# A two-layer DiT in split fp32: x loaded first, the first gate in the first phase, quarter sums of unsplit chunks, and the first values' projections interleaved part by part

## The chip, the cores and the metric

One core of a Trainium2 chip runs the whole program. The metric is the device time of one execution in microseconds. Five engines work side by side, each in its own fixed order: TensorE (PE) for matmuls, VectorE (DVE) and ScalarE (ACT) for element-wise work, GpSimd (POOL), and SyncE (SP), from whose queue the weights are loaded.

## The reference, cut to what matters

Two layers, each a half-step SwiGLU, a token mixer and another half-step SwiGLU, on 512 latent and 256 context tokens of width 1024 (768 rows in all). Each sub-layer takes the root mean square norm of its input and modulates it with shift and scale, and its result is multiplied by a gate; shift, scale and gate are products of a 1024-vector (`c` for latent, `c_ctx` for context tokens) with `ada_w`. All in float32.

```
def layer(x, xc, mod_l, mod_c, pre_wi, pre_wo, post_wi, post_wo, mixer, ctx_out):
    sh1, sc1, g1, sh2, sc2, g2, sh3, sc3, g3 = jnp.split(mod_l, N_MOD, axis=-1)
    ...
    def ffn_step(t, sh, sc, g, wi, wo):
        return t + 0.5 * g * swiglu(modulate(rms(t), sh, sc), wi, wo)

    x = ffn_step(x, sh1, sc1, g1, pre_wi, pre_wo)
    xc = ffn_step(xc, ch1, cc1, cg1, pre_wi, pre_wo)
    o_l, o_c = mixer(h_lat=modulate(rms(x), sh2, sc2), h_ctx=modulate(rms(xc), ch2, cc2), ctx_out=ctx_out)
    x = x + g2 * o_l
    x = ffn_step(x, sh3, sc3, g3, post_wi, post_wo)
    ...
for i in range(DEPTH):                      
    mod_l = (jax.nn.silu(c) @ ada_w[i] + ada_b[i])[:, None, :]
    mod_c = jax.nn.silu(c_ctx) @ ada_w[i] + ada_b[i]
```

## The kernel before

Activations are kept with the width on the partitions: x is 8 chunks (k) of 128 x 768, and a matmul takes a 128x128 piece of a weight as the stationary side and up to 512 tokens as the moving one. Every float32 matmul is done as three products of rounded parts: `h_h` with `whi`, `h_l` with `whi`, `h_h` with `wlo`. A slab of weights (`raw`, 128 x 1024, 512 KB, three places) is loaded through SP, cast on ACT (`whi`, line 73) and subtracted on DVE (`wlo`, line 74).

A feed-forward phase runs over 22 hidden blocks f. Blocks 0, 1 and 2 are plain (line 521): 96 matmuls for the two projections up, 48 of 512 columns and 48 of 256. From f=3 on seven products take the place of eight (class `Seven`, line 454), on sums of quarters of the activations (`T1`, `T2`, `T3`, made in `sums` at f=1) and of the weights (`s`, lines 440 to 443). In `sums` the two parts of a chunk are first added again (`both`, line 418), then the quarters are subtracted (`t`, lines 422 to 425) and split; `t4` replaces a quarter of the activations from f=3 on (`replace`).

Phase 0 starts cold. SP loads the vectors (`crep`, the two conditioning vectors on all partitions), x, and the modulation weights: shift for chunk k (`shift_job`, two sums of 128x1024 on DVE, line 182), scale (`scale_job`, on PE, lines 195 and 199), in one ring of nine places named `araw`. DVE and ACT make the norm (squares line 1117, adds line 1120), then `feed(k)` makes chunk k: product with `rall` (line 1134), modulation on ACT (line 1137), cast `h_h` (line 1138), `h_l` (line 1139), and PE multiplies block 0 chunk by chunk.

The gate of phase 0 (m=2), and all later modulations, are made by `Halves`: for half a column block (512) and chunk d, a load `wh` (line 237) and two sums of 128x512 on DVE (line 240), spread as steps over the hidden blocks from f=1 on; `beside(3, (5, 5, 6))` puts the gate's 16 steps into f=1, 2 and 3. The gate is needed first where phase 0's down projection is added to x (line 386).

In each attention the first projections read the norm's parts as they come out (blocks of 128 tokens, two of them a part of 256 columns): `qk` with heads 0 for all blocks, then `val` for all blocks in attention 0; `keys`, then `values`, in attention 1 (line 670 for the ones that start with the parts, line 657 for the rest). Each of them splits its weights' slabs into the ring of `whi`/`wlo` places.

A scheduler fixes the order of each engine when the program is built, by a model of costs, from the order in which the code is written and from which places are free; on the chip each engine runs that order, and waits for what it needs.

## Time and profile before

| | |
|---|---|
| median of 3 runs | 2842.01 us (2840.68 to 2843.09) |
| the profiled execution | 2840.03 us, span 2838.1 us, granted PE clock 0.987 |
| PE busy | 2701.7 us, 95% |
| DVE busy | 2185.6 us, 77% |
| ACT busy | 1207.4 us, 43% |
| POOL busy | 343.8 us, 12% |
| chain of work that ended last | PE 73%, DVE 14%, DMA 5%, ACT 3% |

The span is the time between the first and the last instruction in the trace; a little lies around it. The busy share is an average over the phases. The chain is followed back from the last instruction, at each step to what released it.

### The profile page before, as it was taken

Reading aid. Unit: us, or ns where it says so; the run is one execution under the profiler, and the core shown is the slowest. Engines: PE = TensorE matmul, PEld = TensorE weight load, DVE = VectorE, ACT = ScalarE, POOL = GpSimd, SP = SyncE. Lnnn points to the kernel's source line nnn. Section 1 sums busy time; section 2 is a strip of 40 time slices with the busy share of each in tenths; the row PEclk is TensorE's granted clock in tenths of the full one; section 3 lists DMA queues with packets and bytes.
Section 4 is the critical chain, followed back from the end, with each engine's and each line's share of the span. In section 5 each row is a group of like instructions: output and inputs, shape, how many; then the busy total and the mean of one; then the engine's idle time right before and its main releaser. Section 6 shows DMA issues by size and latency. Waiting matters only on the chain.

```text
span 2838.1 us, 47439 instructions
## 1 busy us (share of the span) xinstructions
PE 2701.7 (95%) x18028; PEld 2561.8 (90%) x18028; DVE 2185.6 (77%) x4727; ACT 1207.4 (43%) x2999; POOL 343.8 (12%) x468
## 2 busy tenths in 40 slices
PE   5799999989999889999999999999999999999999
PEld 4699998989999878999899989999998999899999
DVE  6988887886777768877787697777778666488887
ACT  4323332355655644332233352333235566444443
POOL 1000000043533421000000100000003421100000
PEclk9899999999999999999999999999999999999999
DMA  6433433321110142332333223432332101232333
GB/s 230 132 117 122 138 101 112 108 97 39 37 40 31 31 137 70 112 106 91 113 122 101 64 64 123 134 123 95 124 112 79 59 16 38 68 97 90 105 97 97
DMA packets 99284, 267.54 MB, mean 94 GB/s; under 512 B 12656, under 2 KB 16752, under 8 KB 98928
## 3 DMA queue, kind: packets, MB, share of 16 engines
q1 hardware_dynamic: 92544, 252.83, 27.8%
q10 hardware_dynamic: 6512, 11.68, 1.3%
q8 instruction: 142, 2.33, 0.3%
q14 instruction: 86, 0.70, 0.1%
HBM read 257.12 MB, written 7.34 MB: 93 GB/s over the span
## 4 chain that ended last, share of the span: by engine, by line
PE 73%; DVE 14%; DMA 5%; ACT 3%; issue 2%; POOL 1%; SPq 0%; ACTq 0%; POOLq 0%; DVEq 0%
PE ps_up L454 26%; PE ps_dn L568 22%; PE ps_qkv L657 7%; PE ps_up L521 5%; PE ps_dn L734 4%; DMA wh<-in_ada_w 3%; DVE wlo L74 2%; PE ps_av L995 2%; DVE wh L240 1%; DMA raw<-in_pre_wi 1%; PE ps_av L831 1%; PE ps_s L787 1%; DVE xs L369 1%; PE ps_pt L984 1%; DVE junkh L240 1%
## 5 line engine op out<-in xcount | busy, mean ns | idle before, releaser
L73 ACT CAST whi<-raw 128x512 fp32r<-128x512 f32 x556 | 341.0, 620 | 661.3 <-PE ps_dn L568 297.6
L568 PE MATMUL ps_dn<-ah,whi 128*128 128x256 f32 (+1 forms) x1456 | 464.6, 322 | 12.4 <-DVE x L386 10.7
L568 PE MATMUL ps_dn<-al,whi 128*128 128x256 f32 (+1 forms) x1456 | 461.9, 320 | 0.1
L568 PE MATMUL ps_dn<-ah,wlo 128*128 128x256 f32 (+1 forms) x1456 | 454.8, 319 | 0.2 <-DVE wlo L74 0.2
L74 DVE TENSOR_TENSOR wlo<-raw,whi 128x512 fp32r<-128x512 f32 x556 | 383.0, 693 | 77.2 <-ACT whi L73 59.6
L454 PE MATMUL ps_up<-h_h,whi 128*128 128x384 f32 (+1 forms) x1216 | 396.6, 326 | 23.0 <-ACT whi L73 16.5
L454 PE MATMUL ps_up<-h_l,whi 128*128 128x384 f32 (+1 forms) x1216 | 394.1, 324 | 0.0
L454 PE MATMUL ps_up<-h_h,wlo 128*128 128x384 f32 (+1 forms) x1216 | 393.3, 324 | 0.0
L386 DVE SCALAR_TENSOR_TENSOR x<-ps_dn,mod,x 128x256 f32<-128x256 f32 (+1 forms) x442 | 240.6, 554 | 129.6 <-PE ps_dn L568 104.8
L568 PEld LDWEIGHTS ps_dn<-ah,whi 128*128 128x128 f32 x1456 | 276.5, 191 | 35.8 <-ACT whi L73 8.2
L73 ACT CAST whi<-s 128x512 fp32r<-128x512 f32 x304 | 188.3, 620 | 272.2 <-PE ps_up L454 224.9
L568 PEld LDWEIGHTS ps_dn<-al,whi 128*128 128x128 f32 x1456 | 277.8, 191 | 19.6 <-DVE al L74 0.3
L568 PEld LDWEIGHTS ps_dn<-ah,wlo 128*128 128x128 f32 x1456 | 276.2, 191 | 20.4 <-DVE wlo L74 0.5
L454 PEld LDWEIGHTS ps_up<-h_h,whi 128*128 128x128 f32 x1216 | 230.4, 189 | 29.3 <-ACT whi L73 17.4
L74 DVE TENSOR_TENSOR wlo<-s,whi 128x512 fp32r<-128x512 f32 x304 | 208.0, 685 | 30.8 <-ACT whi L73 27.7
L454 PEld LDWEIGHTS ps_up<-h_h,wlo 128*128 128x128 f32 x1216 | 229.5, 189 | 1.9 <-DVE wlo L74 1.5
L454 PEld LDWEIGHTS ps_up<-h_l,whi 128*128 128x128 f32 x1216 | 230.3, 189 | 0.5
L657 PE MATMUL ps_qkv<-whi,h_h 128*128 128x256 f32 x704 | 204.6, 291 | 4.3 <-DVE a L613 3.6
L657 PE MATMUL ps_qkv<-wlo,h_h 128*128 128x256 f32 x704 | 199.8, 286 | 0.7 <-DVE wlo L74 0.7
L657 PE MATMUL ps_qkv<-whi,h_l 128*128 128x256 f32 x704 | 200.0, 285 | 0.0
L240 DVE SCALAR_TENSOR_TENSOR wh<-wh,ch 128x512 f32<-128x512 f32 x256 | 173.8, 690 | 19.5 <-DMA wh<-in_ada_w 19.3
L244 POOL TENSOR_TENSOR mod<-mod,part 128x16 f32<-128x16 f32 (+1 forms) x32 | 14.4, 450 | 1428.8 <-DVE wh L240 1428.8
(223 smaller groups left out, 6442.8 us busy)
## 6 DMA issues: line engine op xcount, KB each, us to landing
wh<-in_ada_w SPq DMA_DIRECT2D x256, 256.0 KB, 3.9
raw<-in_pre_wi SPq DMA_DIRECT2D x88, 512.0 KB, 3.5
raw<-in_post_wi SPq DMA_DIRECT2D x88, 512.0 KB, 3.5
raw<-in_pre_wo SPq DMA_DIRECT2D x44, 512.0 KB, 3.5
raw<-in_post_wo SPq DMA_DIRECT2D x44, 512.0 KB, 3.6
raw<-in_a_w_qk SPq DMA_DIRECT2D x16, 512.0 KB, 3.5
araw<-in_ada_w SPq DMA_DIRECT2D x8, 512.0 KB, 9.7
araw<-in_ada_s SPq DMA_DIRECT2D x8, 512.0 KB, 10.2
```

The source lines that it names most:

```text
L73: nc.scalar.copy(hi, src)
L74: nc.vector.tensor_sub(lo, src, hi.bitcast(F32))
L240: nc.vector.scalar_tensor_tensor(o, w, 1.0, self.c[ty], ALU.mult, ALU.mult, accum_out=self.part[:, ty, d:d + 1])
L369: nc.vector.scalar_tensor_tensor(xs, x[:, d, tk], sc, self.r[p], ALU.mult, ALU.mult)
L386: nc.vector.scalar_tensor_tensor(x[:, d, s0:s0 + n], ps, gate[ty][:, d:d + 1], x[:, d, s0:s0 + n], ALU.mult, ALU.add)
L454: nc.tensor.matmul(ps, ww, z[:, k, :n], start=first and k == 0 and i == 0, stop=k == 3 and i == 2, skip_group_check=True)
L521: nc.tensor.matmul(ps, w, h[:, k, s0:s0 + n], start=k == 0 and i == 0, stop=k == KC - 1 and i == 2)
L568: nc.tensor.matmul(ps, wv, a[:, s0:s0 + n], start=fi == 0 and k == 0, stop=fi == nf - 1 and k == 2)
L657: nc.tensor.matmul(ps, h[:, k, bt], w, start=n == 0, stop=n == 23)
L734: nc.tensor.matmul(ps, wv, o[:, k, s0:s0 + n], start=k == 0 and j == 0, stop=k == KC - 1 and j == 2)
L787: nc.tensor.matmul(sv[:, u], Q[:, c, qt], K[:, c, kb0 * P + u * half:kb0 * P + (u + 1) * half], start=i == 0, stop=i == 1)
L995: nc.tensor.matmul(po[:, j], a[:, k, j], V[:, kb, g], start=k == 0, stop=k == len(kbs) - 1)
```

## The change

SP loads the first half of x (512 columns) ahead of the conditioning vectors, and the second half behind them, then shift and scale of the first two chunks in turn. The gate m=2 leaves `Halves`: it is made by eight `vector_job`s, the former `shift_job` with m as an argument, each a load of 128x1024 and two sums of that width, written behind block 0 (`beside` at f=0). `Seven.sums` takes, in phase 0 alone, the modulated chunks `xr`, which still stand in their places unsplit, so the eight `both` adds are gone there, and `t4` is written over the first half of an `xr`. In the attentions `by_parts` puts the first values between the first queries and keys, two blocks at a time; the split weights of these values live in the places that later hold `aT` and `p` (`pT` in attention 1), under the name `vw`. Apart from these, the same instructions run.

```diff
--- before.py
+++ after.py
...
     class Slab:
-        def __init__(self, raw, room=(wp, 4)):
+        def __init__(self, raw, room=(wp, 4), places=None):
             self.parts = []
             for c in range(0, raw.shape[1], 512):
-                hi, lo = (room[0].tile([P, 512], F32R, name=z, tag=z, bufs=room[1]) for z in ("whi", "wlo"))
+                if places is not None:
+                    hi, lo = places.pop(0), places.pop(0)
+                else:
+                    hi, lo = (room[0].tile([P, 512], F32R, name=z, tag=z, bufs=room[1]) for z in ("whi", "wlo"))
                 split(hi, lo, raw[:, c:c + 512])
...
         return raw
-    def load_slab(src, pin=False):
-        return Slab(load_raw(src, pin))
+    def load_slab(src, pin=False, places=None):
+        return Slab(load_raw(src, pin), places=places)
+    def by_parts(f, g):
+        return [(h, 0, b) for p in range(0, NB, 2) for h in (f, g) for b in (p, p + 1)]
     other_banks("psf0")
...
         for ty, nm in enumerate(("c", "c_ctx")):
-            nc.sync.dma_start(crep[:, ty], I[nm].partition_broadcast(P))
+            keep(nc.sync.dma_start(crep[:, ty], I[nm].partition_broadcast(P)))
             nc.scalar.activation(crep[:, ty], crep[:, ty], AF.Silu)
...
     mods = [[None] * NMOD for _ in range(2)]
-    def shift_job(k, pool, crep, bufs):
+    def vector_job(m, k, pool, crep, bufs):
         w = pool.tile([P, D], F32, name="araw", tag="araw", bufs=bufs)
-        keep(nc.sync.dma_start(w, I["ada_w"][0, k]))
-        md = mods[0][0][2][:, :, k]
+        keep(nc.sync.dma_start(w, I["ada_w"][0, m * KC + k]))
+        md = mods[0][m][2][:, :, k]
         def sums():
...
                 nc.vector.scalar_tensor_tensor(o, w, 1.0, crep[:, ty], ALU.mult, ALU.mult, accum_out=md[:, ty:ty + 1])
-            nc.vector.tensor_add(md, md, adab[:, 0, k:k + 1].broadcast_to([P, 2]))
+            nc.vector.tensor_add(md, md, adab[:, 0, m * KC + k:m * KC + k + 1].broadcast_to([P, 2]))
+            if m == 2:
+                nc.vector.tensor_scalar_mul(md, md, 0.5)
         return sums
...
             self.cm.__exit__(None, None, None)
-        def sums(self, pool):
+        def sums(self, pool, full=None):
             n = self.n
-            self.t4 = [pool.tile([P, T], F32, name="t4", tag=tag, bufs=5) for tag in ("ah", "al")]
+            self.t4 = []
+            if full is None:
+                rooms = [pool.tile([P, T], F32, name="t4", tag=tag, bufs=5) for tag in ("ah", "al")]
             for k in range(KC // 2):
...
                 for i, tag in enumerate(("ah", "al")):
-                    r = pool.tile([P, T], F32, name="both", tag=tag, bufs=5)
                     kk = k + i * KC // 2
-                    nc.vector.tensor_add(r[:, :2 * n], self.hi[:, kk, :2 * n].bitcast(F32),
-                                         self.lo[:, kk, :2 * n].bitcast(F32))
+                    if full is None:
+                        r = pool.tile([P, T], F32, name="both", tag=tag, bufs=5)
+                        nc.vector.tensor_add(r[:, :2 * n], self.hi[:, kk, :2 * n].bitcast(F32),
+                                             self.lo[:, kk, :2 * n].bitcast(F32))
+                    else:
+                        r = full[kk]
                     b.append((r[:, :n], r[:, n:2 * n]))
                 t1, t2, t3 = (self.pool.tile([P, 512], F32, name="t", tag="s", bufs=4)[:, :n] for _ in range(3))
+                self.t4.append(rooms[k // 2][:, k % 2 * n:k % 2 * n + n] if full is None else b[1][0])
                 nc.vector.tensor_sub(t1, b[0][1], b[0][0])
...
                 nc.vector.tensor_sub(t3, b[1][1], b[0][1])
-                nc.vector.tensor_sub(self.t4[k // 2][:, k % 2 * n:k % 2 * n + n], b[1][0], t2)
+                nc.vector.tensor_sub(self.t4[k], b[1][0], t2)
                 for (th, tl), t in zip(self.T, (t1, t2, t3)):
...
             for k in range(KC // 2):
-                split(self.hi[:, k, n:2 * n], self.lo[:, k, n:2 * n], self.t4[k // 2][:, k % 2 * n:k % 2 * n + n])
+                split(self.hi[:, k, n:2 * n], self.lo[:, k, n:2 * n], self.t4[k])
         def up(self, pool, wg, wu, ah, al, first):
...
     EARLY = 1
-    def ffn(l, msh, w1, w2, nt, norm, pool, after_up, follow, side, beside=None, between=None, feed=None):
+    def ffn(l, msh, w1, w2, nt, norm, pool, after_up, follow, side, beside=None, between=None, feed=None, full=None):
...
             if f == PLAIN - 2:
-                seven.sums(pool)
+                seven.sums(pool, full)
             ah = pool.tile([P, T], F32R, name="ah", tag="ah", bufs=5)
...
             if pr_ not in vals:
+                places = None
+                if pr_ == 0:
+                    rooms = [pool.tile([P, 3 * 512], F32R, name="vw", tag="aT", bufs=2) for _ in range(2)]
+                    places = [r[:, c:c + 512] for c in range(0, 3 * 512, 512) for r in rooms]
+                    places += [pool.tile([P, T], F32R, name="vw", tag="p", bufs=5)[:, :512] for _ in range(2)]
                 vals[pr_] = (pool.tile([P, NB, 256], F32, name="V", tag="V", bufs=2),
-                             [load_slab(I["a_w_v"][pr_, half]) for half in range(2)])
+                             [load_slab(I["a_w_v"][pr_, half], places=places) for half in range(2)])
             V, slabs = vals[pr_]
...
             return (4, 5, 0, 1, 2, 3) if i else range(NB)
-        order = [(qk, 0), (val, 0), (qk, 1), (val, 1), (qk, 2), (qk, 3), (val, 2), (qk, 4), (qk, 5), (val, 3),
+        order = [(qk, 1), (val, 1), (qk, 2), (qk, 3), (val, 2), (qk, 4), (qk, 5), (val, 3),
                  (qk, 6), (qk, 7)]
-        proj = Projections([((f, i, b), lambda f=f, i=i, b=b: f(i, b)) for f, i in order for b in turns(i)], 2)
+        blocks = by_parts(qk, val) + [(f, i, b) for f, i in order for b in turns(i)]
+        proj = Projections([(fib, lambda fib=fib: fib[0](*fib[1:])) for fib in blocks], 2)
         later = Later()
...
             if b == 0:
-                qs_["v"] = [load_slab(I["b_w_kv"][1, half]) for half in range(2)]
+                rooms = [pool.tile([P, 5 * 512], F32R, name="vw", tag="pT", bufs=2) for _ in range(2)]
+                places = [r[:, c:c + 512] for c in range(0, 4 * 512, 512) for r in rooms]
+                qs_["v"] = [load_slab(I["b_w_kv"][1, half], places=places) for half in range(2)]
             nc.scalar.copy(V[:, b], project(b, hh, hl, qs_["v"]).rearrange("p (g d) -> p g d", g=4))
...
             nc.scalar.copy(O[:, 2 * g:2 * g + 2, qb * P:(qb + 1) * P], pt)
-        order = [(keys, 0, NB), (values, 0, NB)] + [(query, g, 4) for g in range(4)]
-        proj = Projections([((f, i, b), lambda f=f, i=i, b=b: f(i, b)) for f, i, n in order for b in range(n)], 1)
+        blocks = by_parts(keys, values) + [(query, g, b) for g in range(4) for b in range(4)]
+        proj = Projections([(fib, lambda fib=fib: fib[0](*fib[1:])) for fib in blocks], 1)
         later = Later()
...
     nc.scalar.activation(cvec, cvec, AF.Silu)
-    for m in range(2):
+    for m in range(3):
         md = const.tile([P, 2, KC], F32, name=f"mod0_{m}")
...
         load_small()
+        load_x(all_[0])
         crep = ada_vectors(start)
-        shifts = [shift_job(k, start, crep, FIRST) for k in range(2)]
+        load_x(all_[1])
         keep(nc.sync.dma_start(adab, I["ada_b"]))
-        for hf in range(2):
-            load_x(all_[hf])
-        scales = [scale_job(k, start, FIRST) for k in range(2)]
-        for f in shifts:
-            f()
+        first = [(vector_job(0, k, start, crep, FIRST), scale_job(k, start, FIRST)) for k in range(2)]
         xr = [pool.tile([P, T], F32, name="xr", tag=("ah", "al")[d % 2], bufs=5) for d in range(KC)]
...
                 step()
-        for f in scales:
-            f()
+        for z in first:
+            for f in z:
+                f()
         later = {}
...
             if k + 2 < KC:
-                later[k + 2] = [shift_job(k + 2, start, crep, FIRST), scale_job(k + 2, start, FIRST)]
+                later[k + 2] = [vector_job(0, k + 2, start, crep, FIRST), scale_job(k + 2, start, FIRST)]
             hi, lo = h0.reg.hi[:, k], h0.reg.lo[:, k]
...
             h1.open()
-        halves.add(0, (2,))
         halves.add(0, range(3, NMOD - 1))
-        others = halves.beside(3, (5, 5, 6))
+        others = halves.beside(3)
         def beside(f, seven):
             if f == 0:
+                for k in range(KC):
+                    vector_job(2, k, start, crep, FIRST)()
                 start_cm.__exit__(None, None, None)
...
                     others(f, seven)
-        ffn(0, 0, I["pre_wi"][0], I["pre_wo"][0], T, h0, pool, up_done, h1.follow, "right", beside, halves.between(13), feed)
+        ffn(0, 0, I["pre_wi"][0], I["pre_wo"][0], T, h0, pool, up_done, h1.follow, "right", beside, halves.between(13), feed, xr)
     o = attention_phase(0, h1, T)
```

Line numbers of the rows of the changed kernel below are those of its own file: line 190 there is line 182 before, 1161 is 1139, 570 is 554, 438 to 444 are 422 to 428.

SP's queue at the start of the program, before:

```order
L1096 DMA cvec<-in_cvec 128x16
L122 DMA crep<-in_c 128x1024
L122 DMA crep<-in_c_ctx 128x1024
L176 DMA araw<-in_ada_w 128x1024 x2
L1105 DMA adab<-in_ada_b 128x144
L129 DMA x<-in_x 128x4x512 x2
L129 DMA x<-in_x 128x4x256 x2
L190 DMA araw<-in_ada_s 128x1024 x2
L94 DMA raw<-in_pre_wi 128x1024 x2
L176 DMA araw<-in_ada_w 128x1024
```

and now:

```order
L1120 DMA cvec<-in_cvec 128x16
L137 DMA x<-in_x 128x4x512 x2
L130 DMA crep<-in_c 128x1024
L130 DMA crep<-in_c_ctx 128x1024
L137 DMA x<-in_x 128x4x256 x2
L1130 DMA adab<-in_ada_b 128x144
L184 DMA araw<-in_ada_w 128x1024
L200 DMA araw<-in_ada_s 128x1024
L184 DMA araw<-in_ada_w 128x1024
L200 DMA araw<-in_ada_s 128x1024
L97 DMA raw<-in_pre_wi 128x1024 x2
L184 DMA araw<-in_ada_w 128x1024
```

x moved ahead of the vectors and of the first `araw`; the same loads stand ahead of the first two `raw`. Behind them follow, as before, the other twelve `araw` of shift and scale, then now the eight of the gate, and only then the `raw` of block 1.

DVE from the last-but-one `h_l` of block 0 on, before (`sg` is the first gate-and-up product of block 0's result):

```order
L1139 TENSOR_TENSOR h_l<-xr,h_h 128x768
L201 SCALAR_TENSOR_TENSOR mod_1_95<-ps_b,adab 128x2
L1139 TENSOR_TENSOR h_l<-xr,h_h 128x768
L74 TENSOR_TENSOR wlo<-raw,whi 128x512 x2
L554 TENSOR_TENSOR sg<-sg,ps_up 128x512
L74 TENSOR_TENSOR wlo<-raw,whi 128x512
L418 TENSOR_TENSOR both<-h_h,h_l 128x768
L240 SCALAR_TENSOR_TENSOR junkh,part<-wh,ch 128x512
L554 TENSOR_TENSOR sg<-sg,ps_up 128x256
L74 TENSOR_TENSOR wlo<-raw,whi 128x512
```

and now, from the last `h_l` on, first piece:

```order
L1161 TENSOR_TENSOR h_l<-xr,h_h 128x768
L190 SCALAR_TENSOR_TENSOR araw,mod_2_96<-araw,crep 128x1024
L190 SCALAR_TENSOR_TENSOR junk,mod_2_96<-araw,crep 128x1024
L193 TENSOR_SCALAR mod_2_96<-mod_2_96 128x2
L191 TENSOR_TENSOR mod_2_96<-mod_2_96,adab 128x2
L190 SCALAR_TENSOR_TENSOR araw,mod_2_96<-araw,crep 128x1024
L193 TENSOR_SCALAR mod_2_96<-mod_2_96 128x2
L191 TENSOR_TENSOR mod_2_96<-mod_2_96,adab 128x2
L570 TENSOR_TENSOR sg<-sg,ps_up 128x512
L190 SCALAR_TENSOR_TENSOR araw,mod_2_96<-araw,crep 128x1024
L570 TENSOR_TENSOR sg<-sg,ps_up 128x256
```

and a few rows later (`sums` of the first quarter chunk, then the splits of block 1's weights):

```order
L74 TENSOR_TENSOR al<-sg,ah 128x512
L191 TENSOR_TENSOR mod_2_96<-mod_2_96,adab 128x2
L438 TENSOR_TENSOR t<-xr 128x384
L193 TENSOR_SCALAR mod_2_96<-mod_2_96 128x2
L74 TENSOR_TENSOR al<-sg,ah 128x256
L193 TENSOR_SCALAR mod_2_96<-mod_2_96 128x2
L439 TENSOR_TENSOR t<-xr,t 128x384
L440 TENSOR_TENSOR t<-xr 128x384
L438 TENSOR_TENSOR t<-xr 128x384
L444 TENSOR_TENSOR T1l<-t,T1h 128x384
L441 TENSOR_TENSOR xr<-xr,t 128x384
L74 TENSOR_TENSOR wlo<-raw,whi 128x512 x2
```

The splits of block 1's weights (`wlo` from `raw`) stood right behind the last `h_l`; now four sums of the gate, block 0's `sg` and `al` and the first quarter sums stand between. Twelve of the gate's sixteen sums stand ahead of the last `h_l`.

PE at the start of attention 0 (`ps_qkvs` are the first projections, `ps_qkv` the values', `ps_rt` a column sum of the norm), before:

```order
L670 MATMUL ps_qkvs<-whi,h_h 128x256
L670 MATMUL ps_qkvs<-whi,h_l 128x256
L670 MATMUL ps_qkvs<-wlo,h_h 128x256
L670 MATMUL ps_qkvs<-whi,h_h 128x256
L286 MATMUL ps_rt<-ones,ar 128x1 x2
L670 MATMUL ps_qkvs<-whi,h_l 128x256
L670 MATMUL ps_qkvs<-wlo,h_h 128x256
```

and now, about the same place:

```order
L686 MATMUL ps_qkvs<-whi,h_h 128x256
L686 MATMUL ps_qkvs<-whi,h_l 128x256
L686 MATMUL ps_qkvs<-wlo,h_h 128x256
L673 MATMUL ps_qkv<-vw,h_h 128x256 x2
L673 MATMUL ps_qkv<-vw,h_l 128x256
L673 MATMUL ps_qkv<-vw,h_h 128x256 x2
L673 MATMUL ps_qkv<-vw,h_l 128x256
L673 MATMUL ps_qkv<-vw,h_h 128x256 x2
```

The values' products, which stood behind all of the first queries and keys, now stand between them, in pieces of two blocks. In attention 1 the order on PE changes in the same way.

## Rows read from the trace of the kernel before

**Rows 1.** The page, part 1: busy us (share of the span) and instructions of each engine.

```profile
PE 2701.7 (95%) x18028; PEld 2561.8 (90%) x18028; DVE 2185.6 (77%) x4727; ACT 1207.4 (43%) x2999; POOL 343.8 (12%) x468
```

**Rows 2.** Busy time by stretch: stretch, length, PE, PEld, DVE, ACT, POOL, clock, DMA.

```profile
50.00:75.00 25.00, 24.12 (x137) 19.16 (x136) 12.60 (x26) 11.84 (x21) 0.00 (x0) 1.00 0.24 74
71.50:105.28 33.78, 33.78 (x194) 29.38 (x193) 33.48 (x75) 15.39 (x32) 0.40 (x1) 1.00 0.47 145
100.00:125.00 25.00, 9.17 (x53) 8.33 (x52) 24.58 (x61) 8.20 (x18) 0.40 (x1) 0.70 0.29 90
610.00:641.00 31.00, 26.31 (x199) 24.09 (x198) 28.64 (x70) 19.65 (x77) 17.01 (x20) 1.00 0.43 154
641.00:653.00 12.00, 12.00 (x103) 12.00 (x102) 3.67 (x8) 4.90 (x18) 5.08 (x7) 1.00 0.10 39
2168.00:2185.00 17.00, 12.85 (x93) 11.30 (x91) 16.72 (x38) 11.42 (x40) 9.33 (x13) 1.00 0.37 125
2185.00:2190.00 5.00, 5.00 (x29) 4.92 (x29) 5.00 (x14) 1.79 (x4) 0.92 (x2) 0.66 0.02 3
```

**Rows 3.** Timeline of SP's queue at the start: start us, us, instruction, count.

```profile
14.58 0.90 SPq L94 DMA_DIRECT2D raw<-in_pre_wi  x2
...
17.51 0.33 SPq L190 DMA_DIRECT2D araw<-in_ada_s  x1
18.97 0.33 SPq L176 DMA_DIRECT2D araw<-in_ada_w  x1
...
34.27 0.91 SPq L94 DMA_DIRECT2D raw<-in_pre_wi  x2
```

**Rows 4.** The page, part 6, DMA issues: count, KB each, median us to landing.

```profile
araw<-in_ada_w SPq DMA_DIRECT2D x8, 512.0 KB, 9.7
```

**Rows 5.** Timeline of DVE up to 70 us, idle before and its releaser in brackets.

```profile
24.96 1.97 DVE L74 TENSOR_TENSOR wlo<-raw,whi 128x512 fp32r<-128x512 f32 x3 [0.72 <-ACT whi L73]
...
33.31 1.22 DVE L182 SCALAR_TENSOR_TENSOR junk<-araw,crep 128x1024 bf16<-128x1024 f32 x1
34.46 0.08 DVE L182 DVE_READ_ACCUMULATOR junk<-araw,crep 128x1 f32 x1
...
34.60 3.55 DVE L1134 TENSOR_TENSOR xr<-x,rall 128x768 f32<-128x768 f32 x4
...
68.97 0.96 DVE L1139 TENSOR_TENSOR h_l<-xr,h_h 128x768 fp32r<-128x768 f32 x1 [2.24 <-ACT h_h L1138]
69.84 1.29 DVE L74 TENSOR_TENSOR wlo<-raw,whi 128x512 fp32r<-128x512 f32 x2
```

**Rows 6.** Timeline of DVE during block 1.

```profile
73.47 0.69 DVE L240 SCALAR_TENSOR_TENSOR junkh<-wh,ch 128x512 bf16<-128x512 f32 x1
74.08 0.09 DVE L240 DVE_READ_ACCUMULATOR junkh<-wh,ch 128x1 f32 x1
...
75.62 0.55 DVE L422 TENSOR_TENSOR t<-both 128x384 f32<-128x384 f32 x1
76.09 0.69 DVE L240 SCALAR_TENSOR_TENSOR junkh<-wh,ch 128x512 bf16<-128x512 f32 x1
...
77.92 2.69 DVE L418 TENSOR_TENSOR both<-h_h,h_l 128x768 f32<-128x768 f32 x3
```

**Rows 7.** Timeline of PE at the start of block 3.

```profile
105.28 0.34 PE L454 MATMUL ps_up<-h_h,whi 128*128 128x384 f32 x1
...
123.36 0.69 PE L454 MATMUL ps_up<-h_h,whi 128*128 128x384 f32 x1 [15.83 <-ACT whi L73]
...
127.36 0.34 PE L454 MATMUL ps_up<-h_h,wlo 128*128 128x384 f32 x1
```

**Rows 8.** Timeline of PE in attention 0: the longest of five waits, 610 to 641.

```profile
622.02 0.39 PE L670 MATMUL ps_qkvs<-whi,h_l 128*128 128x256 f32 x1 [1.19 <-DVE h_l L371]
```

**Rows 9.** Timeline of PE in attention 1: the two longest waits from 2168 on.

```profile
2174.80 0.39 PE L670 MATMUL ps_qkvs<-wlo,h_h 128*128 128x256 f32 x1 [1.59 <-DVE wlo L74]
...
2184.93 0.38 PE L670 MATMUL ps_qkvs<-whi,h_l 128*128 128x256 f32 x1 [1.47 <-DVE h_l L371]
```

## The prediction

> **What bounds the kernel now.** I read the busy times of the engines first. TensorE (PE) works for 95% of the span [rows 1], so nearly all the time that can be won lies in the few stretches where PE waits, and the next view is the busy time by stretch of time [rows 2]. It shows three such places that the change touches. Between 100 and 125 us PE is busy for 9.17 of 25 us at a granted clock of 0.70. Between 610 and 641 us, where attention 0 begins, it is busy for 26.31 of 31 us (4.7 us idle), and then for all of the next 12 us. Between 2168 and 2185 us, where attention 1 begins, it is busy for 12.85 of 17 us (4.15 us idle), and the 5 us behind that run at a clock of 0.66. The remaining waits are elsewhere, and the change leaves them alone.
>
> The timeline of PE shows the first place closely [rows 7]: the third hidden block ends at 105.28, the seven-product block f=3 issues 12 matmuls, then PE idles for 15.83 us until 123.36, and the next 12 matmuls take until 127.36: 4.0 us, where the twelve before the wait took 2.1, so 1.9 us at half clock (1.2 instead of 2.4 GHz) come on top. The wait ends with an ACT cast of a sum of weights, and VectorE (DVE), which makes that sum, is busy for 24.58 of those 25 us [rows 2]: it is late. Yet it was idle for 12.4 of the 25 us between 50 and 75 [rows 2], in pauses of which the last, 2.24 us, stands ahead of the last `h_l` [rows 5]. So DVE has the time, only before it has the work.
>
> **The change, part by part.**
>
> *x first.* Up to the first weights the queue moves the same bytes in another order, and these weights are waited for: their DMA issued at 14.58 [rows 3], the first `wlo` began at 24.96 [rows 5]. I cost the new order at nothing: the squares and sums of x get done in DVE's pauses before 24.96, and the `h_l` stand behind the splits of these weights anyway. If the first weights landed earlier or later, all of phase 0's start would move with them, by 1 us at most, I estimate, since loads of 512 KB are issued some 1.5 us apart there [rows 3].
>
> *The gate in whole rows.* 32 halves of 128x512 become 16 sums of 128x1024. A half takes 0.61 us until the next instruction starts (73.47 to 74.08) [rows 6], a whole row 1.15 (33.31 to 34.46) [rows 5]: 16 x 1.15 = 18.4 us for 32 x 0.61 = 19.5, so 1.1 us of DVE less. [...]
>
> What matters is where they stand. In the new order 12 of the 16 stand ahead of the last `h_l`, 4 behind it and ahead of the next block's splits (order at DVE above). From 24.96, where DVE is free, to the end of the last `h_l` it now has 4 splits (2.6 us, 0.66 each), 24 sums of 128x1024 (27.6), 8 products with `rall` (7.1 by 3.55 for four), 8 `h_l` of the same shape (7.1) [rows 5] and some 1.6 us of small ones: 46.0, so it ends at about 71.0 instead of 69.84. It no longer pauses. PE's products of block 0 end 1.7 us later.
>
> *Block 1 then waits.* Before, the splits of block 1 came right behind the last `h_l`, at 69.84 [rows 5], and PE ran on: it was busy for all of the 33.78 us from 71.5 to 105.28 [rows 2], which are the two blocks 1 and 2 with 96 matmuls each, so f=0 ended near 71.5. Now the order has 4 sums of the gate (4.6 us), two `sg` and two `al` (1.9), six operations of the quarter sums 128x384 (2.8 by 0.47, which is the step from 75.62 to the next row at 76.09), some 0.3 of small ones and one split (0.6) between them [rows 5, 6]: 10.2 us behind 71.0, so the first `wlo` is ready at 81.2. PE can do two products before it, so block 1 effectively begins at 80.9: 9.4 us late. PE's wait of some 8 us will drop the clock, as the 15.83 us did [rows 7]; I take the same 1.9 us.
>
> *The stall at f=3 goes.* Behind that point DVE has no half sums of the gate in f=1 and f=2 (they took 19.5 us), no `both` adds (8 x 0.9 = 7 us by the three in 2.69) [rows 6], and in its order the sums `s` of the weights stand ahead of the end of block 2. So f=3 goes on without its wait. DVE's slack for this: it was busy for 33.48 of the 33.78 us of blocks 1 and 2 and for 24.58 of the 25 up to 125 [rows 2], and 26 us of that are now gone or done earlier. Startup: 15.83 + 1.9 won, 9.4 + 1.9 lost, so 6.4 us. Bounds: all 17.7 us if block 1 isn't late, 0 if it is late by 15.8.
>
> *First values part by part, attention 0.* Before, the values' 96 matmuls run alone from 641 to 653, with DVE busy for 3.67 of 12 us, and PE's waits, five, come before that, the longest for an `h_l` [rows 2, 8]. Now values stand between the keys' products on PE (order at PE above), and they need only the same `h_l`. DVE's own work before 653 is 28.64 + 3.67 = 32.3 us, PE's 26.31 + 12.0 = 38.3: with the two side by side PE is the bound, and up to 4.7 us go. The four splits of the values' weights (2.6 us) now come earlier on DVE, in front of `h_l`s. The waits at the very start (one split, one `h_l`) are only partly covered, since the first values come just there. I take 3.6, bounds 0 and 4.7.
>
> *Attention 1.* The same with keys and values: 4.15 us of idle time, with 1.59 and 1.47 us as the longest waits [rows 9], and 5 us at a clock of 0.66, which is worth 1.7 us [rows 2]. I take three quarters of both, 4.4; bounds 0 and 5.9.
>
> *Elsewhere* the order of PE, DVE and SP is the same or differs by a few rows under a busy PE: nothing.
>
> Sum: 6.4 + 3.6 + 4.4 = 14.4 us. The profiled execution took 2840.03, so 2825.6; the median of the three runs is 2.0 us above it: **2827.6 us**.
>
> **The rivals.**
>
> (a) *Block 1 isn't late.* If block 1's start holds and f=3's wait goes, startup wins 17.7 and the sum is 26: 2816. For it: 12.4 idle us of DVE could hold most of the 18.4 us of the gate. Against it: the order is fixed, and nothing in it pulls the splits forward.
>
> (b) *The startup's gain is eaten.* Block 1 starts at 87 instead of 81, because block 0 starves PE in between, at half clock, or ACT's casts (`sg`, `ah`, `T1h`) answer late, as DVE's pause for `h_h` shows it can [rows 5]. Then startup gives 0 and 8.0 stay: 2834.
>
> (c) *The attentions don't fill.* If `h_l` remains what PE waits for, with the values' splits in front of it, the idle time only changes place: 2836 with the startup's 6.4 alone, and 2842, as before, together with (b).
>
> (d) *Slower: the gate's loads.* Each waits on SP for a place of `araw`, and the weights of block 1 stand behind all eight on that queue. A load of this kind takes 9.7 us from issue to landing in the startup [rows 4]. If each landed before the next was issued, seven from 34.27 [rows 3] would end at 102, the last `h_l` near 104.5 and block 1 would begin at 115. The case decides from a start at 101: 87.3, where f=3's old stall is used up, plus the attentions' 8.0, plus 5.7; so it gives 5.7 + 14, 2862. Against it: issues stand 1.5 us apart (17.51 and 18.97) while a load takes 9.7 [rows 3, 4], so they overlap, and the places come free from about 45 on. [...]
>
> **How the numbers follow.** Differences within 0.2% (5.7 us, 2836.3 to 2847.7) can't be told from no change. Chances: the forecast 0.50 (2822 to 2832), (a) 0.13, (b) 0.13, (c) alone 0.12, (b) and (c) together 0.05, (d) 0.07. Faster: 0.50 + 0.13 + 0.11 of (b) + 0.07 of (c) = 0.81; same: the rest of (b), (c) and both together, 0.12; slower 0.07. The range 2817 to 2838 leaves out (d), the double case and the outer parts of (a) and (c), about 0.2.
>
> **What would show it.** Right: no wait of PE near 107, and one of 7 to 9 us at the start of block 1, ended by `wlo` or `whi`; DVE without pauses from 25 to 80; PE idle for less than 1.5 us behind 610 and 2168 each. Wrong: block 1 at or before 73 (a); the 13th matmul of f=3 at 123 or later (b); waits for `h_l` of the old size (c); DVE waiting for DMA ahead of a sum of the gate (d).

## The result, and the profile after

The changed kernel took 2823.35 us (median of four runs, 2820.59 to 2823.57) beside 2841.35 us for the kernel before (2839.78 to 2843.09): a ratio of 0.9930 with a 95% interval of 0.9919 to 0.9942, so 18 us or 0.7% faster. The forecast was 2827.6. Of all the runs below one, the fourth of e_gate_again, took 3287.64 us at a granted clock of 0.751; it stands in no median here. The profiled execution took 2823.49 us, its span is 2821.3. The busy times of the engines, in the order of [rows 1] (busy us, share of the span, instructions), hardly moved:

```profile
PE 2705.1 (96%) x18028; PEld 2565.6 (91%) x18028; DVE 2176.2 (77%) x4703; ACT 1205.7 (43%) x2995; POOL 339.3 (12%) x464
```

PE issues the same 18028 matmuls, and what changed is where it waits. Busy time by stretch, in the columns of [rows 2]:

```profile
50.00:75.00 25.00, 19.03 (x115) 14.74 (x112) 25.00 (x57) 10.55 (x18) 0.00 (x0) 1.00 0.47 169
75.00:100.00 25.00, 18.37 (x81) 15.22 (x82) 22.33 (x54) 10.73 (x23) 0.00 (x0) 0.80 0.21 64
100.00:125.00 25.00, 25.00 (x151) 22.80 (x150) 13.35 (x25) 9.96 (x20) 0.00 (x0) 1.00 0.19 66
...
610.00:645.00 35.00, 35.00 (x294) 34.90 (x294) 26.64 (x65) 18.67 (x80) 17.10 (x24) 0.99 0.36 132
...
2162.00:2185.00 23.00, 22.02 (x181) 21.35 (x180) 21.43 (x50) 15.26 (x53) 10.44 (x13) 1.00 0.31 97
```

Between 50 and 75 us DVE was idle for half of the time before and is now busy without a gap; PE fell from 24.12 to 19.03 there. Between 100 and 125 us it is the other way round: PE, which was busy for 9.17, runs through, and DVE has 11.65 us to spare. The stall moved from block 3 to blocks 0 and 1 and became shorter. In the two stretches of the attentions PE now has next to no gap; in attention 0 two waits stand just ahead of that stretch (below).

The timeline of PE at the start (start, duration, matmul, in brackets the idle time ahead of it and what ended that) shows the new waits, and f=3 without one:

```profile
69.42 0.50 PE L537 MATMUL ps_up<-h_l,whi 128*128 128x512 f32 x1 [3.36 <-DVE h_l L1161]
...
72.72 0.50 PE L537 MATMUL ps_up<-h_l,whi 128*128 128x512 f32 x1 [0.92 <-DVE h_l L1161]
...
80.92 0.79 PE L537 MATMUL ps_up<-h_h,whi 128*128 128x512 f32 x1 [6.54 <-ACT whi L73]
...
83.28 0.79 PE L537 MATMUL ps_up<-h_h,wlo 128*128 128x512 f32 x1 [0.71 <-DVE wlo L74]
...
118.73 0.34 PE L470 MATMUL ps_up<-h_h,whi 128*128 128x384 f32 x1
...
120.82 0.34 PE L470 MATMUL ps_up<-h_h,whi 128*128 128x384 f32 x1
```

The last row is f=3's thirteenth matmul, ahead of which PE waited 15.83 us before [rows 7]. It now comes 2.09 us behind the first, and 2.54 us earlier than before, although block 1 starts with a wait.

DVE in the same place (timeline, answers to [rows 5, 6]):

```profile
69.28 1.22 DVE L190 SCALAR_TENSOR_TENSOR araw<-araw,crep 128x1024 f32<-128x1024 f32 x1
70.42 0.08 DVE L190 DVE_READ_ACCUMULATOR araw<-araw,crep 128x1 f32 x1
...
71.71 0.95 DVE L1161 TENSOR_TENSOR h_l<-xr,h_h 128x768 fp32r<-128x768 f32 x1
72.58 1.22 DVE L190 SCALAR_TENSOR_TENSOR araw<-araw,crep 128x1024 f32<-128x1024 f32 x1
...
82.54 1.28 DVE L74 TENSOR_TENSOR wlo<-raw,whi 128x512 fp32r<-128x512 f32 x2
```

No row there has an idle time in front: the splits of block 1's weights start 9.96 us behind the last `h_l`, and all of that is work. PE's wait of 6.54 us itself ends with ACT's cast of these weights, `whi`. In ACT's order that cast stands behind the casts of block 0's result and of the first quarter sum, and these wait for DVE, where the gate's sums come first (timeline of ACT):

```profile
77.01 0.62 ACT L73 CAST ah<-sg 128x512 fp32r<-128x512 f32 x1 [2.44 <-DVE sg L570]
78.49 0.40 ACT L73 CAST ah<-sg 128x256 fp32r<-128x256 f32 x1 [0.86 <-DVE sg L570]
79.84 0.51 ACT L443 CAST T1h<-t 128x384 fp32r<-128x384 f32 x1 [0.94 <-DVE t L438]
80.25 1.14 ACT L73 CAST whi<-raw 128x512 fp32r<-128x512 f32 x2
```

So the gate's sums hold up block 1 twice, by ACT's queue and, 0.71 us more, by DVE's own splits. In SP's queue (timeline) the gate's loads are not what is late:

```profile
44.12 12.41 SPq L184 DMA_DIRECT2D araw<-in_ada_w  x8
56.58 1.51 SPq L97 DMA_DIRECT2D raw<-in_pre_wi  x3
```

All eight are issued by 56.58, and block 1's weights right behind them, 26 us ahead of their split; each of these three loads landed within 7.0 us of its issue.

At the two attentions these are the waits of PE that are left up to 645 and from 2156 to 2185 (timeline), against [rows 8, 9]:

```profile
605.62 0.39 PE L686 MATMUL ps_qkvs<-whi,h_h 128*128 128x256 f32 x1 [1.60 <-ACT whi L73]
607.49 0.58 PE L686 MATMUL ps_qkvs<-wlo,h_h 128*128 128x256 f32 x1 [1.37 <-DVE wlo L74]
...
2163.91 0.38 PE L686 MATMUL ps_qkvs<-wlo,h_h 128*128 128x256 f32 x1 [0.47 <-DVE wlo L74]
2167.44 0.51 PE L673 MATMUL ps_qkv<-vw,h_h 128*128 128x256 f32 x2 [0.43 <-DVE vw L74]
```

The waits for `h_l` are gone from both. Those for the first weights stayed: in attention 1 they are shorter (0.47 us instead of 1.59 for `wlo`, and 0.43 for `vw`), in attention 0 they are 2.97 us together, where before there was one (timeline of PE, before):

```profile
612.41 0.39 PE L670 MATMUL ps_qkvs<-wlo,h_h 128*128 128x256 f32 x1 [0.91 <-DVE wlo L74]
```

The two of attention 0 do not hang on the new order: with the old one there (e_att0, below) they are 0.99 and 1.37 us.

Where the time came from is read by following one instruction of PE that both programs have through both traces: f=3's first matmul, the first matmul of the down projections (`ps_dn` behind f=3), the first norm sum behind phase 0 that PE waits for, each attention's first output product, and the last matmul. Start times in us; the last two columns are experiments below.

| | before | after | after, second execution (e_again) | gate back (e_gate) |
|---|---|---|---|---|
| f=3, first matmul | 105.28 | 118.73 | 117.52 | 103.76 |
| f=3, thirteenth | 123.36 | 120.82 | 119.60 | 105.84 |
| first down product | 147.99 | 143.85 | 142.61 | 129.83 |
| norm sum behind phase 0 | 602.07 | 596.21 | 598.40 | 587.68 |
| output product, attention 0 | 1012.33 | 1003.32 | 1002.75 | 988.87 |
| norm sum ahead of attention 1 | 2157.59 | 2146.78 | 2147.06 | 2132.63 |
| output product, attention 1 | 2415.23 | 2396.68 | 2398.36 | 2382.45 |
| last matmul | 2834.67 | 2817.74 | 2818.41 | 2801.17 |

From the second column against the first: 4.1 us won at the first down product, 5.9 by the end of phase 0, 3.2 more across attention 0 (410.26 to 407.11), 1.8 up to attention 1, 7.7 across its start (257.64 to 249.90), and 1.6 lost behind: 16.9 in all.

One pair of executions says little of a single segment, and the thirteen traces of this case say more. Attention 0, from the norm sum to its output product, takes 400.7 to 407.1 us, 403.4 on average, in the ten with the new order there, and 409.8 to 411.8, 410.6 on average, in the three with the old one (before, e_start, e_att0). Attention 1 takes 249.8 to 254.2, 251.5 on average, in the ten with the new order, and 257.6 to 260.7, 259.1 on average, in the three with the old one (before, e_start, e_att1). In these segments the new order is worth 7.2 and 7.6 us; the attention 0 of the first profile of after is the longest of its ten.

### The profile page after: what moved, and what is told of

Its sections match the earlier page's. It is cut to its first block, busy times and chain, and to the rows that moved or that the text cites. A ratio compares the mean times of both kernels' runs of the same rounds, so it can differ in the third digit from the quotient of the medians.

```text
span 2821.3 us, 47391 instructions
## 1 busy us (share of the span) xinstructions
PE 2705.1 (96%) x18028; PEld 2565.6 (91%) x18028; DVE 2176.2 (77%) x4703; ACT 1205.7 (43%) x2995; POOL 339.3 (12%) x464
## 5 line engine op out<-in xcount | busy, mean ns | idle before, releaser
L673 PE MATMUL ps_qkv<-whi,h_h 128*128 128x256 f32 x608 | 177.8, 292 | 3.2 <-DVE a L629 2.2
L250 DVE SCALAR_TENSOR_TENSOR wh<-wh,ch 128x512 f32<-128x512 f32 x240 | 163.4, 693 | 18.3 <-DMA wh<-in_ada_w 18.2
L673 PE MATMUL ps_qkv<-wlo,h_h 128*128 128x256 f32 x608 | 174.1, 286 | 0.7 <-DVE wlo L74 0.7
L673 PE MATMUL ps_qkv<-whi,h_l 128*128 128x256 f32 x608 | 173.6, 286 | 0.0
```

Source lines behind the costliest of these rows:

```text
L250: nc.vector.scalar_tensor_tensor(o, w, 1.0, self.c[ty], ALU.mult, ALU.mult, accum_out=self.part[:, ty, d:d + 1])
L673: nc.tensor.matmul(ps, h[:, k, bt], w, start=n == 0, stop=n == 23)
```

## The experiments

Theory after the result: the stall at f=3 went because DVE has less to do there; the gate's sums, which stand ahead of block 1's splits, cost most of what that wins; and each attention's order is worth what its segment shows. Rivals: the gate's move is what removed the stall; x first did part of it; the attentions' gains are drift. Each run below changes the changed kernel, and its time stands beside runs of the kernel before on the same chip (medians 2843.97, 2842.56 and 2844.34 in the three groups).

**Both attentions in the old order (e_start).**

```diff
-        order = [(qk, 1), (val, 1), (qk, 2), ...
+        order = [(qk, 0), (val, 0), (qk, 1), (val, 1), (qk, 2), ...
-        blocks = by_parts(qk, val) + [(f, i, b) for f, i in order for b in turns(i)]
+        blocks = [(f, i, b) for f, i in order for b in turns(i)]
...
-                qs_["v"] = [load_slab(I["b_w_kv"][1, half], places=places) for half in range(2)]
+                qs_["v"] = [load_slab(I["b_w_kv"][1, half]) for half in range(2)]
-        blocks = by_parts(keys, values) + [(query, g, b) for g in range(4) for b in range(4)]
+        blocks = [(f, 0, b) for f in (keys, values) for b in range(NB)] + [(query, g, b) for g in range(4) for b in range(4)]
```

(`val` of the first heads takes the common places too.)

> The changed kernel with both attentions in the old order (values behind all of the first queries and keys, their splits in the ring of whi/wlo), so the change at the start alone. If the three places add up as the traces of before and after show them (5.8 us at the end of phase 0), this is about 5.9 us faster than before, 2835.5. If part of the 18 us came by chance of the granted clock in later phases, it lies off that by more than 1.5 us.

Measured: 2833.75 us (2827.73 to 2839.97), ratio to before 0.9961 [0.9947, 0.9975]. The startup alone is faster than before, and the two attentions together are worth 10.4 us against the changed kernel's 2823.35 (8.8 by the ratios, 0.9961 less 0.9930). The time lies 1.75 us below the expected 2835.5, just beyond the 1.5 us that were allowed; with runs of this one kernel 12 us apart that decides nothing about the clock.

**Attention 0 alone in the old order (e_att0).** The edit is the first half of the one above.

> The changed kernel with the old order in attention 0 alone. The prediction has 3.6 us for attention 0, so 2827.0; the cumulative lead in the two traces grows by 6.4 us over the start of attention 0 and falls by 3.3 towards its end, so 2826.5 to 2828; if what PE wins at the start is all given back later in the attention, 2823.4, as the changed kernel.

Measured: 2826.71 us (2822.74 to 2833.19), ratio 0.9942 [0.9925, 0.9959]: 3.4 us more than the changed kernel's 2823.35, where 3.6 was forecast, but 6.3 more than its 2820.37 (e_again), and 7.0 less than e_start in the same group, which is attention 1's share. With runs 10 us apart the time alone does not settle the size; the segments above, 411.79 us here against 403.4 on average, put it nearer 7. In its trace a wait for `h_l` and the one for the norm's `y` are back at the old size (timeline of PE, e_att0):

```profile
616.21 0.38 PE L686 MATMUL ps_qkvs<-whi,h_l 128*128 128x256 f32 x1 [1.18 <-DVE h_l L381]
...
625.47 0.66 PE L657 MATMUL ps_t<-ident,y 128*128 128x128 f32 x4 [1.04 <-POOL y L648]
```

**The gate back beside its halves (e_gate).** x first, unsplit sums and the attentions stay.

```diff
-    for m in range(3):
+    for m in range(2):
...
+        halves.add(0, (2,))
         halves.add(0, range(3, NMOD - 1))
-        others = halves.beside(3)
+        others = halves.beside(3, (5, 5, 6))
...
-                for k in range(KC):
-                    vector_job(2, k, start, crep, FIRST)()
```

> The changed kernel with the gate m=2 back in Halves (32 half sums in blocks 1 to 3); x first, quarter sums of unsplit chunks and the attentions stay. Theory of the prediction: the gate's sums ahead of the splits cost 9.4 us at block 1 and the quarter sums alone take most of the stall at block 3 away (7 us of both adds gone, and the first sums fit into DVE's pauses in block 0), so without the gate's move the start is shorter: no wait of PE at block 1, one of about 4 us at block 3, 2818 (2815 to 2822). Rival: the gate's move is what removes the stall at block 3; then the stall comes back with 12 us or more and the time is 2828 or above.

Measured: 2807.96 us (2804.02 to 2812.0), ratio 0.9874 [0.9859, 0.9889]: faster than the changed kernel by 15 us, well beyond what was expected. The theory's direction holds, but the wait of 4 us that it left at block 3 is not there, and the rival falls: the stall at f=3 does not need the gate's move to go away. f=3's first and thirteenth matmul (timeline of PE, e_gate):

```profile
103.76 0.34 PE L470 MATMUL ps_up<-h_h,whi 128*128 128x384 f32 x1
...
105.84 0.34 PE L470 MATMUL ps_up<-h_h,whi 128*128 128x384 f32 x1
```

PE by stretch in e_gate:

```profile
50.00:75.00 25.00, 22.81 (x128) 17.87 (x127) 18.23 (x40) 16.14 (x30) 0.00 (x0) 1.00 0.22 74
75.00:100.00 25.00, 25.00 (x145) 21.74 (x144) 24.03 (x59) 9.47 (x19) 0.22 (x1) 1.00 0.46 146
100.00:125.00 25.00, 23.91 (x142) 22.93 (x141) 23.89 (x58) 11.17 (x22) 0.00 (x0) 1.00 0.49 145
```

DVE is nearly full from 75 to 125, and PE is too.

**Block 1's weights split ahead of the gate's sums (e_splits).** The gate stays in phase 0; only the place in the program where block 1's two slabs are loaded and split moves.

```diff
-            ws = []
-            for gu in range(2):
+            ws = ready.pop(f, [])
+            for gu in range(len(ws), 2):
                 ws.append(load_slab(w1[f, gu], feed is not None and f < PINNED))
...
+            if feed is not None and f == 0:
+                ready[1] = [load_slab(w1[1, gu], True) for gu in range(2)]
             if beside is not None:
                 beside(f, seven)
```

> The changed kernel with the weights of block 1 loaded and split ahead of the gate's jobs in the program (the gate stays in phase 0). Theory: PE waits at block 1 because the splits stand behind the gate's sums on DVE; two of the four splits now stand ahead of the last h_l and the other two behind four sums of the gate, so PE's wait at block 1 falls from 7.3 us to about 2, the clock stays up, and the time is 2816 (2813 to 2819). Rival: block 1 waits for its weights' loads, or for the places of block 0's weights; then the wait stays and the time is within 1.5 us of 2823.4.

Measured: 2813.19 us (2812.37 to 2814.4), ratio 0.9893 [0.9878, 0.9907], as expected: 10.2 us less than the changed kernel with all of its work. No wait of PE above 0.4 us stands between 72.24, where block 0 still waits for `h_l`, and f=3, whose first matmul starts at 107.57 (118.73 in the changed kernel). So the larger part of what the gate's sums cost is their place ahead of the casts and splits of these weights. The rest remains: PE waits in block 0 for `h_l` (timeline of PE, e_splits),

```profile
63.21 0.50 PE L539 MATMUL ps_up<-h_l,whi 128*128 128x512 f32 x1 [2.12 <-DVE h_l L1165]
...
72.24 0.51 PE L539 MATMUL ps_up<-h_l,whi 128*128 128x512 f32 x1 [2.99 <-DVE h_l L1165]
```

and four sums of the gate stand on DVE between the last two `h_l`. In e_gate the waits there are 1.53 and 0.56 us, f=3 starts 3.8 us earlier than here, and the time is 3.6 to 5.2 us less (2809.60 and 2807.96).

**Gate back, and the sums from split chunks again (e_gate_both).** The edit of e_gate, and

```diff
-        ffn(0, 0, ..., beside, halves.between(13), feed, xr)
+        ffn(0, 0, ..., beside, halves.between(13), feed)
```

> The gate of m = 2 is back beside its halves and the quarter sums of unsplit chunks are undone (both halves' sums from both rows, as before); x first and the two attentions' new order stay. Theory: it is the unsplit sums that take the long wait at f = 3's weights away, so here it comes back, of about 15 us, and the time is 2829 us (2826 to 2833). Rival: x first and the parts' projections took it away; then the time is that of the run with only the gate back, 2808 us (2805 to 2812), with no wait above 2 us there.

Measured: 2830.73 us (2826.73 to 2832.45), ratio 0.9952 [0.9935, 0.9969]: as the theory had it (2826 to 2833), and 21 to 23 us more than e_gate (2807.96, and 2809.60 in its repetition below). The wait is back at f=3 (timeline of PE, e_gate_both):

```profile
102.89 0.34 PE L470 MATMUL ps_up<-h_h,whi 128*128 128x384 f32 x1
...
120.97 0.69 PE L470 MATMUL ps_up<-h_h,whi 128*128 128x384 f32 x1 [15.84 <-ACT whi L73]
```

The cause stands on DVE: the first of the sums of f=3's weights (`s`), here in e_gate_both (timeline of DVE),

```profile
112.78 0.69 DVE L456 TENSOR_TENSOR s<-raw 128x512 f32<-128x512 f32 x1
```

and in e_gate, with the fourth of them (timeline of DVE):

```profile
91.45 0.70 DVE L456 TENSOR_TENSOR s<-raw 128x512 f32<-128x512 f32 x1
...
97.70 0.71 DVE L459 TENSOR_TENSOR s<-raw,s 128x512 f32<-128x512 f32 x1
```

With unsplit sums it stands 21 us earlier, and its fourth part is done before PE reaches f=3 at 103.76. Counted between 60 us and that row, DVE does 11 half sums of modulations there and 22 in e_gate_both (11 x 0.61 = 6.7 us), no `both` instead of eight (7.0), and 10 subtractions of splits instead of 18 (4.2): 17.9 of the 21.3 us; 2.7 more are idle time, 6.8 us instead of 4.1. The `both` themselves are a third of it; the order, made from what is ready when, also puts other work behind the `s`. In e_gate the quarter sums start ahead of the last `h_l`, since they no longer need the split of their chunk (timeline of DVE):

```profile
63.45 0.56 DVE L438 TENSOR_TENSOR t<-xr 128x384 f32<-128x384 f32 x1
...
66.86 0.95 DVE L1161 TENSOR_TENSOR h_l<-xr,h_h 128x768 fp32r<-128x768 f32 x1
```

**The sums from split chunks again, gate in phase 0 (e_both).** Only the one line above.

> Only the unsplit sums are undone in the changed kernel; the gate stays in the first phase. Theory: with the gate's work gone from block 1 VectorE has room there, so that the longer sums push f = 1 by 1 to 2 us and the rest is taken up; 2825 us (2823 to 2829). Rival: the sums are worth as much beside a moved gate as without it; then the 15 us wait at f = 3 comes on top, 2838 us.

Measured: 2822.14 us (2817.66 to 2823.93), ratio 0.9924 [0.9909, 0.9939]: no change against the changed kernel, and 8.6 us less than e_gate_both in the same group. Block 1 starts late by the same kind of waits, and f=3 has none between its first and its thirteenth matmul (timeline of PE, e_both):

```profile
78.32 0.80 PE L537 MATMUL ps_up<-h_h,whi 128*128 128x512 f32 x1 [4.70 <-ACT whi L73]
...
83.20 0.80 PE L537 MATMUL ps_up<-h_h,wlo 128*128 128x512 f32 x1 [1.94 <-DVE wlo L74]
...
116.97 0.34 PE L470 MATMUL ps_up<-h_h,whi 128*128 128x384 f32 x1
...
119.05 0.34 PE L470 MATMUL ps_up<-h_h,whi 128*128 128x384 f32 x1
```

So each of the two edits takes the stall away by itself, and once the gate is moved no gain of the unsplit sums is left that these runs show.

**x in its old place (e_xlast).**

```diff
         load_small()
-        load_x(all_[0])
         crep = ada_vectors(start)
-        load_x(all_[1])
+        shifts = [vector_job(0, k, start, crep, FIRST) for k in range(2)]
         keep(nc.sync.dma_start(adab, I["ada_b"]))
+        for hf in range(2):
+            load_x(all_[hf])
```

(The scales' jobs follow, and the four are called as before the change.)

> Only x first is undone in the changed kernel. Theory: nothing that ends last hangs on x, so 2823 us (2820 to 2826), no change against the changed kernel. Rival: the chunk's end, on which the h_l of block 1 hangs, comes later by the length of x's load, and block 1 with it: 2827 us or above.

Measured: 2821.77 us (2819.36 to 2825.05), ratio 0.9926 [0.9911, 0.9941]: no change, and f=3's first matmul at 118.52 instead of 118.73. Underneath it is not the same course: the last `h_l` ends at 75.94 instead of 72.58, but only two sums of the gate stand behind it instead of four, and the first split of block 1's weights comes at 83.47 instead of 82.54.

**Gate back and x in its old place (e_gate_xlast).** Both edits together.

> The gate of m = 2 is back beside its halves and x is loaded in its old place; the unsplit sums and the attentions' new order stay. Theory: x first is worth nothing, since what ends last at the start comes behind it; 2808 us (2805 to 2811), within 3 us of the run with only the gate back. Rival: x first wins the first chunk's time; then 2812 us or above.

Measured: 2811.38 us (2804.92 to 2813.22), ratio 0.9884 [0.987, 0.9899]. Beside e_gate's 2807.96 and 2809.60 this decides nothing. In the traces f=3's first matmul starts at 106.75, in e_gate at 103.76 and in its repetition at 104.80: x first may be worth 2 to 3 us there, where no wait stands behind it. That is not settled.

**The changed kernel again (e_again),** with no edit.

> The changed kernel once more, with nothing altered. In its first profile attention 0 was 6.4 us ahead of before at one point and gave 3.3 us back late, in waits at half clock that the kernel before doesn't have. Theory: that loss belongs to the execution and not to the program, so here attention 0, from the end of the first phase to its first output projection, takes 401 to 404 us instead of 407.1, and the median time is 2823 us (2820 to 2826). Rival: it belongs to the order of the change; then attention 0 takes 407 us again.

Measured: 2820.37 us (2819.21 to 2824.17), ratio 0.9920 [0.9905, 0.9935]. Attention 0 took 404.35 us from the norm sum to its output product, 0.35 us above the theory's band and 2.8 us below the rival's 407.1. So the larger part of what the first profile gave back there belongs to that execution; the other eight traces with this order in attention 0, at 400.7 to 404.3, say the same. The median 2820.37 is as expected (2820 to 2826).

**Attention 1 alone in the old order (e_att1).** The edit is the second half of that of e_start.

> Only attention 1's order is undone in the changed kernel: keys first, then all values, whose weights lie in the common places again. Theory: that order is worth the 7.7 us that the trace shows between the start of attention 1 and its first output projection, so 2831 us (2828 to 2834). Rival: it is worth the 4.4 us of the forecast, 2828 us, and the rest was drift.

Measured: 2828.15 us (2823.45 to 2830.99), ratio 0.9943 [0.9927, 0.9960]. The absolute number fits both theories, since the changed kernel took 2820.37 in this group and not 2823.4; the difference is 7.8 us, with runs 7.5 us apart here and 5 us in e_again, so the time alone does not part 7.7 from 4.4. The trace speaks for the theory: 258.92 us from the norm sum to the output product against 251.30 in e_again, and 7.6 us by all thirteen traces. The two waits for `h_l` are back (timeline of PE, e_att1):

```profile
2158.54 0.39 PE L686 MATMUL ps_qkvs<-whi,h_l 128*128 128x256 f32 x1 [1.11 <-DVE h_l L381]
...
2166.78 0.39 PE L686 MATMUL ps_qkvs<-whi,h_l 128*128 128x256 f32 x1 [1.46 <-DVE h_l L381]
```

**The gate back, again (e_gate_again),** the kernel of e_gate with no further edit, beside e_again.

> The kernel with only the gate of m = 2 back beside its halves, once more with nothing altered, next to the changed kernel. Theory: the gate's move costs 15 us in the presence of the unsplit sums: 2808 us (2804 to 2812) beside 2823. Rival: the earlier distance was partly a difference between chips or batches, and here it is 10 us or less.

Measured: 2809.60 us (median of three, 2809.39 to 2811.82), ratio 0.9879 [0.9860, 0.9899]. That is 10.8 us below e_again, between the theory's 15 and the rival's 10. Against before, in ratios, the move costs 0.56% (0.9930 less 0.9874) in the first comparison and 0.41% in this one; in the traces f=3's thirteenth matmul is 12.7 us (119.60 less 106.88) to 15.0 us later with it. I take 10 to 15 us.

The four combinations of the two edits, with all else as in the changed kernel (median us):

| | gate beside its halves | gate in phase 0 |
|---|---|---|
| sums from split chunks | 2830.73 | 2822.14 |
| sums from unsplit chunks | 2807.96, 2809.60 | 2823.35, 2820.37 |

The best version is the lower left one, 1.2 to 1.3% faster than the kernel before.

## Why the prediction was right, step by step

**The stall at f=3: right in size, half of its reason too many.** 15.83 + 1.9 us were to go; 16.0 went between the first and the thirteenth matmul (18.08 to 2.09 us), and 1.6 behind it, up to the first down product (24.63 to 23.03). The prediction counted both relieving edits, 19.5 us of half sums and 7 us of `both`, and took their sum for the slack. The 19.5 us were read too high: of the 32 half sums 22 stood ahead of f=3's sums `s` before (13.4 us), so some 20 us were freed there and not 26. Either edit alone is enough (e_gate, e_both). The prediction asked whether the sum covers the need, and not which of the two would have covered it alone, so it did not see that the stall would go without the gate's move and its cost.

**Block 1's wait: right in place and size, the half clock behind it too short, and ACT overlooked.** The forecast was 9.4 + 1.9 = 11.3 us; f=3's first matmul is 13.45 us later in the first profile and 10.8 to 13.5 in the five with this startup (after, e_again, e_start, e_att0, e_att1). Block 1 begins at 80.92, where 80.9 was forecast. The 2.1 us are lost behind that: 37.8 us pass from there to f=3 instead of 33.8 [rows 2]. Of the 4.0 us 0.71 are the wait for `wlo`, and most of the rest is half clock, for which the forecast took 1.9 from [rows 7], where it was over 4.0 us behind the wait (granted clock 0.51 from 123.36 to 127.36, before). The traces give the clock as a share: the forecast's 1.2 GHz agrees with 384 columns of a matmul every 0.32 us behind that wait, and its 2.4 is twice that, an estimate, where 384 columns every 0.17 us (2.2 per ns) are measured ahead of it. Here it lasts longer, with a clock of 0.50 from 79 to 88 us (busy time by stretch, after):

```profile
79.00:88.00 9.00, 6.37 (x15) 4.91 (x16) 9.00 (x22) 4.47 (x10) 0.00 (x0) 0.50 0.23 62
```

That 80.92 meets 80.9 so closely is in part luck. The splits stand 9.96 us behind the end of the last `h_l`, where 9.6 was forecast up to their start, and that end lies at 72.58 and not at 71.0 (70.9 to 72.6 in the five), of which 1.1 us is the first `wlo` of f=0, at 26.05 instead of 24.96 [rows 5], the 1 us that the prediction allowed for x first. But the first matmul needs only `whi`, and its wait ends with ACT's cast, which the prediction's sum does not have. PE waited in block 0 too, 3.36 and 0.92 us. The sums themselves were priced right: 1.22 us each, 1.15 from one to the next, as in [rows 5]. DVE kept to its order: the weights had landed by 65.1 (issued by 58.1, 7.0 us at most) and the first `whi` was ready at 80.9, and yet DVE started three more operations of the quarter sums, at 81.14, 81.60 and 82.07, before the split at 82.54.

**Startup: 6.4 forecast, 4.1 to 6.9 measured** at the first down product in the five profiles with this startup, 5.3 on average.

**x first at nothing: right** for this kernel (e_xlast). It holds, but not by the course that the prediction gave: with x in its old place block 0 ends later, and block 1 then waits less behind it (e_xlast). With the gate's sums away it is open (e_gate_xlast).

**Attention 0: the mechanism right, the term about half of what it is.** 3.6 forecast, with 4.7 as the bound; 3.2 by the first profile's segment (407.11 against 410.26), which is the longest of its ten, 7.2 by the averages of all thirteen, 3.4 to 6.3 by e_att0's time. The waits at the first weights stayed, as the prediction said, but at 2.97 us, so its sign of less than 1.5 us of idle time is not met if the stage is counted from its first weights on. Counted on PE's timeline from the norm sum, the 300th matmul comes 4.0 us earlier in the first profile and 4.7 in the second; the rest comes behind, where the prediction had looked at nothing.

**Attention 1: the mechanism right, the term too small.** Three quarters of 5.9 us were taken, 4.4; measured were 7.7 and 6.3 by segment, 7.6 by the averages of all thirteen traces, 7.8 by e_att1, 7.0 by e_start less e_att0. Counted on PE's timeline from the norm sum, the 300th matmul comes 5.5 us earlier than before (42.3 instead of 47.8), nearly all of the bound: both waits for `h_l` go, and that for the first `wlo` shrinks from 1.59 to 0.47; 2.2 us more come behind it, where the prediction had looked at nothing. What these are, and the like in attention 0, was not taken apart.

**The rivals.** (a), block 1 in time, did not happen by itself, and e_splits, with block 1 in time, gives 2813, even better than its 2816. (b) and (c) did not come about: f=3's thirteenth matmul lies before 123, and the waits for `h_l` are gone. (d) is refuted by SP's queue: eight loads of the gate in 12.41 us, and no sum of the gate waits for a DMA.

**The sum.** 14.4 us were forecast from one profile to the other; the table gives 16.9: startup 5.9 for 6.4, attention 0 3.2 for 3.6, attention 1 7.7 for 4.4, and elsewhere 1.8 won and 1.6 lost where nothing was forecast. In this pair attention 1 is the whole difference. By the averages above the three terms are 5.3, 7.2 and 7.6, some 20 us, and the ratio of e_again (0.9920) says 23: that the first profile came so close to the forecast is in part its slow attention 0. The rest of the 4 us between 2827.6 and 2823.35 is that the forecast was carried to the median of before, 2.0 us above its profile, and the profile of after lies at its own median.

## What to carry to other kernels

When two edits cure the same wait, price each alone before adding them: here either one was enough to remove 16 us, and the gate's move then only kept its own cost. An engine with idle time ahead of a wait is not free space, because in a fixed order the work put there stands in front of everything written behind it (with the splits ahead of the gate's sums e_splits took 10.2 us less); write first what the next stage waits for (the casts and splits, on each engine that makes them), then the work that can be late (the gate, which is needed only at phase 0's end). And look for operands that exist earlier than those used: the quarter sums of unsplit chunks need no `both` and start ahead of the last split. How much each of the two gave was not taken apart.
